# Both halves of a modulation row in one spread, and five reorderings of issue

## The chip, the cores and the metric

The kernel runs on one core of a Trainium2 chip. The metric is the device time of one execution in microseconds. Three runs of the kernel before gave 704.02, 704.18 and 706.19; the median is 704.18. One more execution was profiled.

The names of the profile: PE is TensorE's matmuls, PEld its weight loads, DVE is VectorE, ACT is ScalarE, POOL is GpSimd, SP is SyncE, which here issues DMAs. A "q" behind a name is the sequencer of that engine. Line numbers (L778) are lines of the kernel before.

## The reference

One layer of a decoder trunk on 512 tokens of width 1024, all in float32. A vector c gives six modulation rows: silu(c) times w_ada, a sum over 1024 rows of a matrix, plus a bias.

```python
mod = cs @ w_ada[l] + b_ada[l]
shift1, scale1, gate1, shift2, scale2, gate2 = split(mod, 6)
h = rmsnorm(x, norm1_g) * (1 + scale1) + shift1
qa, ka, va, qd, kd, vd, ga, gd = split(h @ w_in)
out_a = sliding_window_attention(qa, ka, va)       # 8 heads, window 128
out_d = diff_attention(qd, kd, vd)                 # 4 heads, two softmaxes, per-head norm
merged = sigmoid(ga) * (out_a @ w_branch_swa) + sigmoid(gd) * (out_d @ w_branch_diff)
x = x + gate1 * (merged @ w_out)
h2 = rmsnorm(x, norm2_g) * (1 + scale2) + shift2
a, g = split(h2 @ w_up)                            # 2 x 2816 columns
x = x + gate2 * ((gelu(causal_conv3(a) + conv_b) * g) @ w_down)
out = rmsnorm(x, final_g)
```

## The kernel before

**Precision.** Matrix products are made of three fp32r matmuls: a high part, rounded, and a low part, the rest, of both operands (high by high, high by low, low by high). So each weight and each activation is first split: a copy on ScalarE writes the high part, a subtraction on VectorE the low part. TensorE waits for the one that comes last, mostly the low part.

**The stages, in order of time.** The input is normalised and shift1 and scale1 are made (to about 60 us); the projection and, between its pieces, the two attentions run to about 317 us, with their gates and branch projections; the output projection to about 362; then "the merge", which closes the output projection, normalises again and opens the up projection; the up projection to about 590, by products of sums of quarter blocks named p1, m5, m6, p2, p3, m7, p4 (`mul_slot`, L1142, matmuls at L1150); the down projection by the same seven products, one pass of six groups each, in the order m1, m5, m6, p2, p3, m7, p4 (`multiply`, L1754, matmuls at L1759), and at the end the last residual and the final norm (`last_rows`, L1695).

**Modulation rows.** The other four rows (gate1, shift2, scale2, gate2) are made beside the attentions by VectorE. `ada_rows` (L764) is a generator: for each row `idx` and each half `hf` of 512 columns it goes through w_ada in four loads of two 128-row blocks (`ada_load`, L757, 512 KB each, issued by SyncE into one of the four buffers of `raw_tile`, L105, which the weights of the projections use too), and adds block times entry of silu(c) into a 128x512 tile `arow`: one multiply (L776) for the first block and a multiply-add (L778) for each of the other seven. The tile of half 0 has the tag `sq2`, that of half 1 the tag `g2b1`; each tag is one buffer. What is left is the sum over the 128 partitions. `ada_spread` (L785) does it with a matrix of ones on TensorE: four matmuls (L789), each with 32 columns of ones and 128 columns of `arow`, each at its own column tile of the array and into its own 32 partitions of a PSUM bank (`tbank`, L99, two banks shared with all transposes). ScalarE copies the result (L794), and a DMA from GpSimd (L795) writes one row of each 32 to DRAM, from where the rows are read later. A float32 matmul is two instructions in the profile, so a spread is eight.

`fill` (L489) issues pieces of projections between the steps of attention, and on each eighth call takes one step of `ada_rows`; `after` (L514) holds the spread back by one more call. From the 20th call on the operations of a row are given a higher priority than what is issued around them, but less than the row copy has. A scheduler then orders each engine's instructions by priority and dependence; each engine issues its own in that order. TensorE's order is written by hand in this part.

**The merge** (L1368 to L1480) and `last_rows` are written out by hand for all of TensorE, VectorE, ScalarE and GpSimd: the order of the lines is the order of issue on each engine. In the merge `sum_w`, `cast_w` and `low_w` (L1081 to L1093) make a sum of weight blocks (VectorE), its high part (ScalarE) and its low part (VectorE) for block column J; `turn2` (L1241) transposes the normalised input on TensorE, `mod_one` (L1250, activation at L1255) applies scale2 and shift2 to it on ScalarE; `mul_slot` is a product; `behind` (L1172) moves a product's result on (VectorE or ScalarE); `conv_taps` (L1159) is two multiply-adds of VectorE, `conv_gelu` an activation of ScalarE.

**The down projection** takes for each pass the six groups `g`, and for each group the two row blocks `u` of 128 tokens. The last pass, p4, holds its last three groups back for `last_rows`, which takes u = 0, then u = 1 in two halves of the columns, and closes the rows: multiply by the gate (L1671), add (L1674), square with its sum (L1677, ScalarE), multiply by the final gain (L1681), the power -1/2 on GpSimd (L173) between small VectorE steps (L171, L179, L183), and two scalings (L1688 on VectorE, L1692 on ScalarE), each with its output DMA.

Of the kernel before, what the change touches and what calls it, by code (L numbers as in the profile page):

```python
# [53 lines left out]
def kernel(  # L54
# [44 lines left out]
    def tbank(name, shape=(P, S)):  # L99
        return bank("t", 2, list(shape), name)  # L100
# [413 lines left out]
    def after(n, fn):  # L514
        later.append([n, fn])
# [241 lines left out]
    def ada_load(idx, hf, k):  # L757
        c0 = (2 + idx) * D + hf * S
        r = raw_tile([P, 2, S], f"ra{idx}{hf}_{k}")
        nc.sync.dma_start(r, wada[k * P : (k + 2) * P, c0 : c0 + S].rearrange("(a p) n -> p a n", p=P))  # L760
        return r


    def ada_rows():  # L764
        todo = [(idx, hf, k) for idx in range(4) for hf in range(2) for k in range(0, KT, 2)]
        r = ada_load(*todo[0])
        yield
        for (idx, hf, k), job in zip(todo, todo[1:] + [None]):
            nxt = ada_load(*job) if job else None
            if k == 0:  # L770
                ac = big.tile([P, S], F32, tag=("sq2", "g2b1")[hf], name=f"arow{idx}{hf}")
            with tc.high_priority(offset=HP // 2) if tick[0] > ADA_EASY else ExitStack():
                for a in range(2):
                    cc = cs[:, k + a : k + a + 1]
                    if k + a == 0:
                        nc.vector.tensor_scalar_mul(ac, r[:, a], cc)  # L776
                    else:
                        nc.vector.scalar_tensor_tensor(ac, r[:, a], cc, ac, ALU.mult, ALU.add)  # L778
            if k == KT - 2:
                after(ADA_LAG, lambda idx=idx, hf=hf, ac=ac: ada_spread(idx, hf, ac))  # L780
            r = nxt
            yield


    def ada_spread(idx, hf, ac):  # L785
        pr = tbank(f"pr{idx}{hf}", (P, P))
        for g in range(4):
            gs = slice(32 * g, 32 * g + 32)
            nc.tensor.matmul(  # L789
                pr[gs], ones[:, gs], ac[:, g * P : (g + 1) * P], start=True, stop=True, tile_position=(0, 32 * g)  # L790
            )
        row = big.tile([P, P], F32, tag="g2b0", name=f"row{idx}{hf}")
        with tc.high_priority(offset=HP):
            nc.scalar.copy(row, pr)  # L794
        nc.gpsimd.dma_start(  # L795
            mod_rows[idx, hf * S : (hf + 1) * S].rearrange("(g n) -> g n", g=4), row[0:P:32]
        )


    pair_w = {}  # L800
# [280 lines left out]
    def sum_w(J, name):  # L1081
        src = R[J, SRC[name]]
        nc.vector.tensor_add(src, src, R[J, "a11" if name == "m6" else "a12"])  # L1083

    def cast_w(J, name):
        W[J, name] = [
            wp.tile([P, 4, 256], F32R, tag=g, bufs=WB, name=f"{name}_{J}_{g}") for g in ("whi", "wlo")
        ]
        nc.scalar.copy(W[J, name][0], R[J, SRC[name]])  # L1089

    def low_w(J, name):
        hi, lo = W[J, name]
        nc.vector.tensor_sub(lo, R[J, SRC[name]], hi.bitcast(F32))  # L1093
# [61 lines left out]
    def conv_bias(J, u):  # L1155
        j = 2 * J + u
        nc.scalar.activation(grow(j), av[J][:, u], AF.Identity, bias=cv[:, 66 + j : 67 + j], scale=cv[:, 44 + j : 45 + j])  # L1157
# [92 lines left out]
    def mod_one(dst, tp, g, kk, on_vector=False):  # L1250
        k = 2 * g + kk
        if on_vector:
            nc.vector.tensor_scalar(dst[:, kk], tp[:, kk], a2c[:, k : k + 1], s2c[:, k : k + 1], ALU.mult, ALU.add)
        else:
            nc.scalar.activation(dst[:, kk], tp[:, kk], AF.Identity, bias=s2c[:, k : k + 1], scale=a2c[:, k : k + 1])  # L1255

    def ks(g):
        return slice(2 * (g % 2), 2 * (g % 2) + 2)
# [108 lines left out]
    g22 = pairs2.rearrange("p (b u n) -> p b u n", b=2, u=2)  # L1367
    tps = {g: turn2(2, g) for g in (0, 1)}  # L1368
    mul_slot(0, "p2", (0,))
    cast_w(0, "m5")  # L1370
    for g in (0, 1):
        for kk in range(2):
            mod_one(b12[:, ks(g)], tps[g], g, kk)
    for g in (2, 3):
        tps[g] = turn2(2, g)
    mul_slot(0, "p2", (1,))
    mul_slot(1, "p1", (1,))
    mul_slot(1, "p2")
    bV += [tbank("up6"), tbank("up7")]
    low_w(0, "m5")  # L1380
    for q in (q0, q1):
        V.tensor_sub(t1n[:, q], b11[:, q], b12[:, q])
    sum_w(0, "m6")
    hi_t(0, t1n, q0)
    for kk in range(2):
# [47 lines left out]
    mul_slot(1, "m6")  # L1433
    behind(1, "m5")
    conv_bias(0, 1)
    conv_taps(0, 0)
    sum_w(1, "p3")
    conv_taps(0, 1)
    cast_w(1, "p3")
    conv_gelu(0, 0)  # L1440
    behind(1, "m6")
    cast_w(1, "m7")
    low_w(1, "p3")
    mul_slot(1, "p3")
    conv_gelu(0, 1)
    low_w(1, "m7")
# [2 lines left out]
    cast_w(2, "p1")  # L1449
    behind(0, "c22")  # L1450
    behind(0, "p4")
    behind(1, "p2")
    low_w(2, "p1")
    mul_slot(2, "p1")
    behind(1, "p3")
    cast_w(1, "p4")
# [238 lines left out]
    def last_rows(todo):  # L1695
        man = ExitStack()
        man.enter_context(
            tc.manual_schedule(engines={nc.vector.engine, nc.scalar.engine, nc.tensor.engine, nc.gpsimd.engine})
        )
        c0, c1 = slice(0, H), slice(H, S)  # L1700
        part = [partial(parts[2 + u, 1]) for u in range(2)]
        for g in todo:
            multiply(len(passes) - 1, g, 0)
        for sl in (c0, c1):
            for g in todo:
                multiply(len(passes) - 1, g, 1, sl)
        for u in range(2):
            nc.scalar.activation(x1[:, u], x1[:, u], AF.Copy, scale=stat_end(u))
            nc.sync.dma_start(od[u * P : (u + 1) * P, :], x1[:, u])
        last_mul(0)  # L1710
        s0 = last_add(0)
        last_gain(0)
        last_mul(1, c0)
        r0 = rstd_start(s0, 1, D, bp, plus=part[0])
        s1 = last_add(1, c0)
        last_gain(1, c0)
        rs0 = bp.tile([P, 1], F32, tag="rs2", bufs=4, name="rse0")
        rstd_end(rs0, *r0, 1, bp)
        partial(s1, part[1])
        last_mul(1, c1)  # L1720
        s2 = last_add(1, c1)
        r1 = rstd_start(s2, 1, D, bp, plus=s1)
        last_gain(1, c1)
        last_scale(0, rs0)
        last_scale2(0, rs0, nc.sync)
        rs1 = bp.tile([P, 1], F32, tag="rs2", bufs=4, name="rse1")
        rstd_end(rs1, *r1, 1, bp)
        last_scale(1, rs1)
        last_scale2(1, rs1, nc.scalar)
        man.close()  # L1730
# [37 lines left out]
    for i in range(len(passes)):  # L1768
        for g in range(NG):
            prepare(i, g)  # L1770
            for _ in range(EACH.get(i, (0,) * NG)[g]):
                next(tasks)()
        tail = HOLD if i == len(passes) - 1 else 0
        for g in range(NG - tail):
            for u in range(2):
                multiply(i, g, u)
        if tail:
            last_rows(range(NG - tail, NG))
        else:
            tasks = after_pass(passes[i][0])  # L1780
            if i < 2:
                for _ in tasks:
                    pass
# [27 lines left out]
```

## Time and profile before

| | us |
|---|---|
| median of three runs | 704.18 |
| profiled execution | 704.88 |
| its span, first to last instruction | 703.0 |
| TensorE busy | 683.2 (97%) |
| VectorE busy | 571.9 (81%) |
| ScalarE busy | 375.5 (53%) |
| GpSimd busy | 82.3 (12%) |
| TensorE's mean granted clock | 0.994 |

How to read it. The profiled execution's own time is 1.9 us more than its span, and 0.70 more than the median. Lines of the timeline give start, duration, engine, line of the kernel, operation, output and inputs, shapes and, in brackets, how long the engine stood idle in front of it and which instruction ended that. A group line gives the operation, its count, its busy time, the mean of one in ns, and the idle time in front of the group. TensorE's matmuls overlap in the records: the step from start to start, not the duration, is what one costs.

### The profile page before, as it was taken

The page shows a single profiled execution, that of the slowest core. Times are in us where ns is not written, and L with a number is a line of the kernel's source. Part 1 is how long each engine was busy: PE and PEld are TensorE (multiplying, and loading weights), DVE is VectorE, ACT ScalarE, POOL GpSimd, SP SyncE. Part 2 cuts the span into 40 slices and gives each one's busy share as a digit, 9 for nine tenths or more (in the row PEclk, how much of TensorE's full clock was granted, in tenths as well). Part 3 has the DMA queues.
Part 4 walks back from the last instruction along what each step waited for, and adds up shares of the span by engine and source line. Part 5 has one row for each costly group of instructions (what it writes and reads, how often), then busy time and mean ns, then how long its engine had stood idle before and what let it go on. Part 6 is the DMA issues. An engine that isn't in the chain of part 4 may idle for free. (4 is left out here: it accounts for less than half of the span.)

```text
span 703.0 us, 11254 instructions
## 1 busy us (share of the span) xinstructions
PE 683.2 (97%) x4203; PEld 595.3 (85%) x4203; DVE 571.9 (81%) x1098; ACT 375.5 (53%) x668; POOL 82.3 (12%) x100
## 2 busy tenths in 40 slices
PE   6999999999999999999999999999999999999994
PEld 5777776778788888888889999999999999888884
DVE  5899886887885557664589898888888999979996
ACT  3646767455452333331468566655565666656664
POOL 3000000001001000000030111111111102530300
PEclk9999999999999999999999999999999999999998
DMA  9885454354435676229517798786889647996803
GB/s 312 282 260 174 150 151 151 92 170 128 134 108 158 194 225 202 96 106 275 185 44 149 188 212 204 169 206 194 197 213 231 156 148 204 196 198 192 157 1 119
DMA packets 115862, 121.81 MB, mean 173 GB/s; under 512 B 4383, under 2 KB 93280, under 8 KB 115808
## 3 DMA queue, kind: packets, MB, share of 16 engines
q1 hardware_dynamic: 96894, 95.09, 42.5%
q0 software_dynamic: 18720, 25.73, 21.7%
q8 instruction: 33, 0.54, 0.3%
q10 hardware_dynamic: 194, 0.28, 0.1%
q14 instruction: 21, 0.17, 0.1%
HBM read 118.97 MB, written 2.11 MB: 172 GB/s over the span
## 5 line engine op out<-in xcount | busy, mean ns | idle before, releaser
L1150 PE MATMUL up<-t,m_whi 128*128 128x256 f32 x528 | 96.1, 283 | 0.0
L1150 PEld LDWEIGHTS up<-t,m_whi 128*128 128x128 f32 x528 | 82.4, 192 | 0.0
L1150 PE MATMUL up<-t,m_wlo 128*128 128x256 f32 x264 | 74.7, 283 | 0.1
L1150 PE MATMUL up<-bh,p_wlo 128*128 128x256 f32 x232 | 65.7, 284 | 0.6 <-DVE p_wlo L1093 0.6
L1150 PE MATMUL up<-bh,p_whi 128*128 128x256 f32 x232 | 65.6, 283 | 0.0
L1150 PE MATMUL up<-bl,p_whi 128*128 128x256 f32 x232 | 65.6, 283 | 0.0
L778 DVE SCALAR_TENSOR_TENSOR arow<-ra,cs,arow 128x512 f32<-128x512 f32 x56 | 41.9, 748 | 21.7 <-DMA ra<-in_w_ada_dram 21.3
L1150 PEld LDWEIGHTS up<-t,m_wlo 128*128 128x128 f32 x264 | 50.6, 192 | 0.3 <-DVE m_wlo L1093 0.3
L1150 PEld LDWEIGHTS up<-bh,p_wlo 128*128 128x128 f32 x232 | 44.4, 192 | 1.0 <-DVE p_wlo L1093 1.0
L1150 PEld LDWEIGHTS up<-bl,p_whi 128*128 128x128 f32 x232 | 44.5, 192 | 0.0
L1150 PEld LDWEIGHTS up<-bh,p_whi 128*128 128x128 f32 x232 | 44.5, 192 | 0.0
L1061 POOL DMA_DIRECT2D s<-in_w_up_dram x21 | 27.0, 1360 | 143.2 <-DMA s<-in_w_up_dram 80.9
L1093 DVE TENSOR_TENSOR m_wlo<-s,m_whi 128x1024 fp32r<-128x1024 f32 x31 | 37.7, 1218 | 2.0 <-ACT m_whi L1089 2.0
L1089 ACT CAST m_whi<-s 128x1024 fp32r<-128x1024 f32 x31 | 32.4, 1046 | 9.4 <-DVE s L1083 5.9
L1150 PE MATMUL up<-t,p_whi 128*128 128x256 f32 x176 | 32.2, 283 | 0.0
L173 POOL TENSOR_TENSOR r<-ms,mhalf 128x1 f32<-128x1 f32 (+1 forms) x16 | 12.6, 788 | 134.3 <-DVE ms L171 75.7
L795 POOL DMA_DIRECT2D mod_rows<-row x8 | 5.1, 643 | 196.7 <-ACT row L794 196.7
L1150 PEld LDWEIGHTS up<-t,p_whi 128*128 128x128 f32 x176 | 27.4, 192 | 0.2 <-issue 0.2
L698 ACT ACTIVATE sd<-sd,dmx 128x128 f32<-128x128 f32 (+3 forms) x32 | 17.7, 556 | 18.5 <-DVE dmx L690 18.5
L1157 ACT ACTIVATE gT<-a,cv 128x512 f32<-128x512 f32 x22 | 17.7, 813 | 17.7 <-DVE a L1192 17.3
L1089 ACT CAST p_whi<-wa 128x1024 fp32r<-128x1024 f32 x18 | 18.7, 1040 | 12.0 <-PE up L1150 10.8
L1150 PE MATMUL up<-t,p_wlo 128*128 128x256 f32 x88 | 24.9, 283 | 0.0
(473 smaller groups left out, 2054.1 us busy)
## 6 DMA issues: line engine op xcount, KB each, us to landing
ra<-in_w_ada_dram SPq DMA_DIRECT2D x32, 512.0 KB, 3.9
wa<-in_w_up_dram SPq DMA_DIRECT2D x22, 512.0 KB, 4.1
s<-in_w_up_dram SPq DMA_DIRECT2D x21, 512.0 KB, 4.8
s<-in_w_up_dram POOLq DMA_DIRECT2D x21, 512.0 KB, 7.8
adaw<-in_w_ada_dram SPq DMA_DIRECT2D x16, 512.0 KB, 5.3
w<-in_w_in_dram SPq DMA_DIRECT2D x12, 512.0 KB, 4.0
a<-in_w_up_dram SPq DMA_DIRECT2D x11, 512.0 KB, 4.6
b<-in_w_down_dram SPq DMA_DIRECT2D x10, 512.0 KB, 3.5
```

The source lines that it names most:

```text
L173: nc.gpsimd.tensor_tensor(r0, ms, mhalf[:, :n], ALU.pow)
L698: exp = nc.scalar.activation(pm[m], pm[m], AF.Exp, bias=mx[:, m : m + 1], scale=slope, accum_out=lsum[:, m : m + 1])
L778: nc.vector.scalar_tensor_tensor(ac, r[:, a], cc, ac, ALU.mult, ALU.add)
L795: nc.gpsimd.dma_start(mod_rows[idx, hf * S : (hf + 1) * S].rearrange("(g n) -> g n", g=4), row[0:P:32])
L1061: nc.gpsimd.dma_start(dst, upblock(*blk), accum_op=ALU.add)
L1089: nc.scalar.copy(W[J, name][0], R[J, SRC[name]])
L1093: nc.vector.tensor_sub(lo, R[J, SRC[name]], hi.bitcast(F32))
L1150: nc.tensor.matmul(o[u], w[:, k, cu], b[:, k], start=name in ("p1", "m5", "p2") and k == 0 and x == 0, stop=k == 3 and x == 2, skip_group_ ...
L1157: nc.scalar.activation(grow(j), av[J][:, u], AF.Identity, bias=cv[:, 66 + j : 67 + j], scale=cv[:, 44 + j : 45 + j])
```

## The change

Six parts, in the order of the code.

1. `ada_spread` is called once for a row, behind its second half, with both halves. It issues eight matmuls, four for each half, into two 128-column pieces of one bank; the row copy is 128x256; two DMAs follow. The accumulation of each column tile is begun by the first half's matmul and closed by the second's.
2. In the merge, `cast_w(0, "m5")` goes behind the first of the two pairs of modulations.
3. There too, `low_w(0, "m5")` goes between the two halves of the t1n subtraction.
4. The sum, the high and the low part of (1, p3) go ahead of the convolution's taps, one pair of taps each; `low_w(2, "p1")` goes ahead of `behind(1, "p2")`.
5. In `last_rows` the norm of the third row block is closed, and its ScalarE scaling issued, before the last multiply; the two column halves of the fourth row block's multiply and add follow each other, and gains, the partial sum and the third block's VectorE scaling come behind.
6. In the last pass but one, m7, the last two groups are issued first for u = 0, then for u = 1.

```diff
@@ -763,6 +763,7 @@
 
     def ada_rows():
         todo = [(idx, hf, k) for idx in range(4) for hf in range(2) for k in range(0, KT, 2)]
+        sums = [None, None]
         r = ada_load(*todo[0])
         yield
         for (idx, hf, k), job in zip(todo, todo[1:] + [None]):
@@ -776,25 +777,29 @@
                         nc.vector.tensor_scalar_mul(ac, r[:, a], cc)
                     else:
                         nc.vector.scalar_tensor_tensor(ac, r[:, a], cc, ac, ALU.mult, ALU.add)
-            if k == KT - 2:
-                after(ADA_LAG, lambda idx=idx, hf=hf, ac=ac: ada_spread(idx, hf, ac))
+            sums[hf] = ac
+            if hf and k == KT - 2:
+                after(ADA_LAG, lambda idx=idx, acs=tuple(sums): ada_spread(idx, acs))
             r = nxt
             yield
 
 
-    def ada_spread(idx, hf, ac):
-        pr = tbank(f"pr{idx}{hf}", (P, P))
-        for g in range(4):
-            gs = slice(32 * g, 32 * g + 32)
-            nc.tensor.matmul(
-                pr[gs], ones[:, gs], ac[:, g * P : (g + 1) * P], start=True, stop=True, tile_position=(0, 32 * g)
-            )
-        row = big.tile([P, P], F32, tag="g2b0", name=f"row{idx}{hf}")
+    def ada_spread(idx, acs):
+        pr = tbank(f"pr{idx}", (P, 2, P))
+        for hf, ac in enumerate(acs):
+            for g in range(4):
+                gs = slice(32 * g, 32 * g + 32)
+                nc.tensor.matmul(
+                    pr[gs, hf], ones[:, gs], ac[:, g * P : (g + 1) * P], start=hf == 0, stop=hf == 1,
+                    tile_position=(0, 32 * g), skip_group_check=True,
+                )
+        row = big.tile([P, 2, P], F32, tag="g2b0", name=f"row{idx}")
         with tc.high_priority(offset=HP):
             nc.scalar.copy(row, pr)
-        nc.gpsimd.dma_start(
-            mod_rows[idx, hf * S : (hf + 1) * S].rearrange("(g n) -> g n", g=4), row[0:P:32]
-        )
+        for hf in range(2):
+            nc.gpsimd.dma_start(
+                mod_rows[idx, hf * S : (hf + 1) * S].rearrange("(g n) -> g n", g=4), row[0:P:32, hf]
+            )
 
 
     pair_w = {}
@@ -1367,19 +1372,20 @@
     g22 = pairs2.rearrange("p (b u n) -> p b u n", b=2, u=2)
     tps = {g: turn2(2, g) for g in (0, 1)}
     mul_slot(0, "p2", (0,))
-    cast_w(0, "m5")
     for g in (0, 1):
         for kk in range(2):
             mod_one(b12[:, ks(g)], tps[g], g, kk)
+        if g == 0:
+            cast_w(0, "m5")
     for g in (2, 3):
         tps[g] = turn2(2, g)
     mul_slot(0, "p2", (1,))
     mul_slot(1, "p1", (1,))
     mul_slot(1, "p2")
     bV += [tbank("up6"), tbank("up7")]
+    V.tensor_sub(t1n[:, q0], b11[:, q0], b12[:, q0])
     low_w(0, "m5")
-    for q in (q0, q1):
-        V.tensor_sub(t1n[:, q], b11[:, q], b12[:, q])
+    V.tensor_sub(t1n[:, q1], b11[:, q1], b12[:, q1])
     sum_w(0, "m6")
     hi_t(0, t1n, q0)
     for kk in range(2):
@@ -1433,14 +1439,14 @@
     mul_slot(1, "m6")
     behind(1, "m5")
     conv_bias(0, 1)
+    sum_w(1, "p3")
     conv_taps(0, 0)
-    sum_w(1, "p3")
+    cast_w(1, "p3")
+    low_w(1, "p3")
     conv_taps(0, 1)
-    cast_w(1, "p3")
     conv_gelu(0, 0)
     behind(1, "m6")
     cast_w(1, "m7")
-    low_w(1, "p3")
     mul_slot(1, "p3")
     conv_gelu(0, 1)
     low_w(1, "m7")
@@ -1449,8 +1455,8 @@
     cast_w(2, "p1")
     behind(0, "c22")
     behind(0, "p4")
+    low_w(2, "p1")
     behind(1, "p2")
-    low_w(2, "p1")
     mul_slot(2, "p1")
     behind(1, "p3")
     cast_w(1, "p4")
@@ -1710,19 +1716,19 @@
         last_mul(0)
         s0 = last_add(0)
         last_gain(0)
-        last_mul(1, c0)
         r0 = rstd_start(s0, 1, D, bp, plus=part[0])
-        s1 = last_add(1, c0)
-        last_gain(1, c0)
         rs0 = bp.tile([P, 1], F32, tag="rs2", bufs=4, name="rse0")
         rstd_end(rs0, *r0, 1, bp)
-        partial(s1, part[1])
+        last_scale2(0, rs0, nc.sync)
+        last_mul(1, c0)
+        s1 = last_add(1, c0)
         last_mul(1, c1)
         s2 = last_add(1, c1)
+        last_scale(0, rs0)
+        partial(s1, part[1])
         r1 = rstd_start(s2, 1, D, bp, plus=s1)
+        last_gain(1, c0)
         last_gain(1, c1)
-        last_scale(0, rs0)
-        last_scale2(0, rs0, nc.sync)
         rs1 = bp.tile([P, 1], F32, tag="rs2", bufs=4, name="rse1")
         rstd_end(rs1, *r1, 1, bp)
         last_scale(1, rs1)
@@ -1771,8 +1777,12 @@
             for _ in range(EACH.get(i, (0,) * NG)[g]):
                 next(tasks)()
         tail = HOLD if i == len(passes) - 1 else 0
-        for g in range(NG - tail):
+        twins = 2 if i == len(passes) - 2 else 0
+        for g in range(NG - tail - twins):
             for u in range(2):
+                multiply(i, g, u)
+        for u in range(2):
+            for g in range(NG - tail - twins, NG - tail):
                 multiply(i, g, u)
         if tail:
             last_rows(range(NG - tail, NG))
```

## The prediction

> **What bounds the kernel now.** I read the page from the top first. One engine is full: TensorE works through 97% of the span, VectorE through 81%. So only two things can move the time: TensorE instructions that come or go, and the places where TensorE stands and waits.
>
> ```profile
> PE 683.2 (97%) x4203; PEld 595.3 (85%) x4203; DVE 571.9 (81%) x1098; ACT 375.5 (53%) x668; POOL 82.3 (12%) x100
> ```
> ```profile
> L778 DVE SCALAR_TENSOR_TENSOR arow<-ra,cs,arow 128x512 f32<-128x512 f32 x56 | 41.9, 748 | 21.7 <-DMA ra<-in_w_ada_dram 21.3
> ```
>
> The second fence is the one to remember. The modulation rows cost VectorE 56 multiply-adds of 0.75 us, plus one short multiply of 0.48 at the head of each half, and before them VectorE already stands 21.3 us for their loads. That is slack only as long as these operations can start early.
>
> Next I read the waits of TensorE, and around each the timeline. The waits that the change touches are quoted below at their parts. All sums are made against the profiled execution (704.88 us, its span 703.0 of them), which is 0.70 above the median of the three runs, 704.18. About 0.3% (2.1 us) is what a measurement of this kernel can tell from no change.
>
> **Part 1, the spreads: what goes.** A spread is 8 short TensorE instructions (4 column tiles, two passes each) between ordinary matmuls. The first fence is the group of all eight spreads, the second one of them in the timeline:
>
> ```profile
> L789 PE MATMUL pr<-arow,ones x64: 272/285/298, 109.1 to 291.4; 128*32 128x128 f32 x64
> ```
> ```profile
> 222.22 0.39 PE L120 MATMUL pA<-outal,wba_h 128*128 128x512 f32 x1
> 222.45 0.39 PE L121 MATMUL pA<-outah,wba_l 128*128 128x512 f32 x1
> 222.77 0.43 PE L789 MATMUL pr<-arow,ones 128*32 128x128 f32 x8
> 223.12 0.50 PE L119 MATMUL pA<-outah,wba_h 128*128 128x512 f32 x1
> 223.46 0.39 PE L120 MATMUL pA<-outal,wba_h 128*128 128x512 f32 x1
> ```
>
> The usual step from one matmul to the next is 0.23 us (222.22 to 222.45). From 222.45 to 223.46 there would be two steps, 0.46; there are 1.01. A spread costs 0.55. Of the eight, four go, one at each first half. The four that stay get 8 more instructions. Their price isn't in the trace: it lies between nothing (they pack beside the others) and 0.55 (a second spread). I take 0.25, twice the 0.12 step of a 256-column matmul (396.88 to 397.00, quoted in part 2), because most of the 0.55 lies at the two edges. So three of the four pairs gain 0.30 each, 0.9 in all.
>
> The first pair is different, since the row copy of its first half stands in front of TensorE:
>
> ```profile
> 111.93 0.48 DVE L776 TENSOR_SCALAR arow<-ra,cs 128x512 f32<-128x512 f32 x1
> 112.17 0.26 ACT L794 COPY row<-pr 128x128 f32<-128x128 f32 x1
> 112.33 0.68 DVE L429 TENSOR_TENSOR qkv<-pv,qkv 128x512 fp32r<-128x512 f32 x1
> 112.49 0.42 PEld L595 LDWEIGHTS tp<-ident,st 128*128 128x128 f32 x4 [1.07 <-ACT row L794]
> ```
>
> TensorE waits for that copy (1.07 in front of the weight load of its transposes), and four transposes later for the qkv low part, which ends at 113.01. Without the copy the second wait is next: its VectorE operation moves up by the arow multiply in front of it (0.40), so the gain is 0.40, not 1. With the larger spread at 136.07 behind it TensorE stands at -0.15.
>
> **Part 1, what it adds: a wait.** The row of a first half lies in a tile with one buffer. Before, the 111.93 multiply could begin the next index's row as soon as the first half had been spread, at 109. Now both halves are read by one spread at 136.07, so in the changed kernel's order of issue this multiply, the two multiply-adds on each of the loads, and all loads that wait for buffers that they release, stand behind it. VectorE issues in order; what is queued behind is the softmax of the diff attention, for which TensorE waits.
>
> ```profile
> 136.07 0.42 PE L789 MATMUL pr<-arow,ones 128*32 128x128 f32 x8
> ```
> ```profile
> DMA to landing us min/median/max: 3.6/3.7/4.1
> ```
> ```profile
> 140.77 0.28 DVE L680 CUSTOM_DVE_ANT_0 sd<-sd,ddf 128x128 f32<-128x128 f32 x1
> ```
> ```profile
> 145.55 0.30 PE L716 MATMUL td<-ident,sd 128*128 128x128 f32 x1
> ```
>
> **Stall A.** The larger spread ends at 136.07 - 0.40 + 0.42 + 0.25 = 136.35, the multiply 0.5 later at 136.9, the first multiply-add at 137.65. This frees the load buffer for the third load of the row, which lands 3.7 later (second fence), at 141.4. Its multiply-add (to 142.2) stands ahead of the scores of query block 1, which started at 140.77 and took 1.27 with their maxima; now they end at 143.4. Between them and the L704 operation that ends them before the transpose at 145.55 the new order has, besides that chain's own small steps (L690, L701, L702 at 0.16 each, 0.3 and 0.35 for L703 and L704, 0.68 for an aTl): three multiply-adds of 0.75 and one multiply of 0.48. That is 4.5, less 0.08 of overlap at each of ten seams, 3.7: 147.1. The transpose starts 0.1 later, 147.2 in place of 145.55: TensorE is at +1.65.
>
> **Stall B.** The scores of query block 2 need the low part of the new keys:
>
> ```profile
> 160.73 0.68 DVE L429 TENSOR_TENSOR qkv<-pk,qkv 128x512 fp32r<-128x512 f32 x1
> 161.33 0.47 DVE L703 TENSOR_SCALAR sd<-sd,dls 128x512 f32<-128x512 f32 x1
> 161.72 0.55 DVE L429 TENSOR_TENSOR aTl<-td,aTh 128x384 fp32r<-128x384 f32 x1
> 162.19 0.74 DVE L704 SCALAR_TENSOR_TENSOR sd<-sd,dls,sd 128x512 f32<-128x512 f32 x1
> ```
> ```profile
> 161.81 0.44 PE L126 MATMUL sd<-qkv 64*128 64x128 f32 x4
> ```
> ```profile
> 150.05 1.23 DVE L116 TENSOR_TENSOR w_l<-w,w_h 128x1024 fp32r<-128x1024 f32 x1 [0.91 <-ACT w_h L115]
> ```
>
> Before, the low part ends at 161.41 and TensorE wants it at 161.98 (the later matmuls of the second fence). In the new order the three operations behind it in the first fence stand ahead of it (1.5 with overlaps), and so do two multiply-adds more than before (2 x 0.67). This stretch starts at the weight split of 150.05 (third fence), for which VectorE already stood waiting on ScalarE, which follows TensorE there; so it starts 1.65 late. The low part ends at 161.41 + 1.65 + 1.5 + 1.35 = 165.9, TensorE starts at 166.1: +4.1, of which 2.45 are new. The later three pairs give back 0.9. In the stages of the third and fourth row I followed the new order by the same durations and found no wait that ends after TensorE's own arrival, though some by only 0.6 us. Part 1: **+3.2**.
>
> The low point of TensorE's activity in B may cost more than its length:
>
> ```profile
> 11.40:14.80 3.40, 1.43 (x13) 0.99 1.10 349
> 14.80:18.10 3.30, 3.30 (x16) 0.50 1.09 350
> ```
>
> These are stretches of the start: length, TensorE busy, granted clock. After 3.4 us with 1.43 busy and no single gap over 1.5 the clock was halved for the next 3.3. The Trainium skill, "TensorE: Matmul & The Clock Gate", section "HAM oscillation — how this bites in real kernels", asks for more: idle of over about 3.4 us. By that page B stays free of charge; by this row it might not. I keep it out of the sum and make it a rival.
>
> **Part 2, the merge.** Moving the cast of m5 behind the first pair of modulations takes away what ScalarE did while it waited for TensorE's transposes:
>
> ```profile
> 367.00 1.03 PE L1245 MATMUL th<-ident,xn 128*128 128x128 f32 x8
> ```
> ```profile
> 367.30 1.03 ACT L1089 CAST m_whi<-s_t 128x1024 fp32r<-128x1024 f32 x1
> 368.24 1.91 ACT L1255 ACTIVATE braw<-th,c 128x256 f32<-128x256 f32 x4
> ```
> ```profile
> 370.20 0.66 PE L1245 MATMUL th<-ident,xn 128*128 128x128 f32 x4 [0.25 <-ACT braw L1255]
> ```
> ```profile
> 391.05 0.48 PE L1150 MATMUL up<-t,p_whi 128*128 128x256 f32 x2
> ```
>
> The first four of the eight transposes are there at about 367.6; ScalarE, free at 367.3, then idles some 0.3, and the cast's full 1.03 falls between the two pairs. The last modulation ends 0.35 later, and so does the transpose at 370.20. The t1n and low operations of VectorE follow, with no gap up to the operation that the matmul at 391.05 waits for; it is 0.6 late: +0.6 instead of nothing. In return, three waits shrink:
>
> ```profile
> 396.88 0.28 PE L1150 MATMUL up<-bh,p_whi 128*128 128x256 f32 x1
> 397.00 0.28 PE L1150 MATMUL up<-bl,p_whi 128*128 128x256 f32 x1
> 397.58 0.39 PE L1150 MATMUL up<-bh,p_wlo 128*128 128x256 f32 x1 [0.31 <-DVE p_wlo L1093]
> ```
> ```profile
> 400.31 0.40 PE L1150 MATMUL up<-t,m_whi 128*128 128x256 f32 x2
> 400.82 0.39 PE L1150 MATMUL up<-t,m_wlo 128*128 128x256 f32 x1
> ```
> ```profile
> 403.68 0.28 PE L1150 MATMUL up<-bl,p_whi 128*128 128x256 f32 x1
> 404.29 0.39 PE L1150 MATMUL up<-bh,p_wlo 128*128 128x256 f32 x1 [0.32 <-DVE p_wlo L1093]
> ```
>
> Start to start beyond the 0.12 step: 0.47, 0.27 (two matmuls in the row) and 0.48. The low part of p3 moves ahead of two taps of 0.75, that of p1 ahead of several 0.33 steps of the closing work of p2, both more than the waits, so they go whole: -1.22. Part 2: **-0.6**.
>
> **Part 3, the end.** Finishing one row block of m7 early ends the wait of p4 for the subtraction:
>
> ```profile
> 678.63 0.47 PE L1759 MATMUL dc<-p4wh,p4a 128*128 128x512 f32 x1 [0.19 <-DVE chain_outl L1633]
> ```
> ```profile
> 694.73 0.65 POOL L173 TENSOR_TENSOR r<-ms,mhalf 128x1 f32<-128x1 f32 x1 [16.07 <-DVE ms L171]
> 697.69 0.62 POOL L173 TENSOR_TENSOR r<-ms,mhalf 128x1 f32<-128x1 f32 x1 [2.30 <-DVE ms L171]
> ```
>
> 678.63 moves to 678.28, a step of 0.23: TensorE ends 0.35 earlier. That isn't passed on: the third row block's power (694.73) now goes first, and its inputs, fixed by VectorE, let it end at about 693.9; two small steps later, at 694.2, the last multiply starts, against 694.10 before. From there multiply, add, multiply, add stand back to back (0.45 each), the last square starts at 696.0 against 696.84, and the second power and all behind it follow 0.85 to 0.95 earlier. Part 3: **-0.9**.
>
> Sum: +3.2 - 0.6 - 0.9 = **+1.7**, 706.6 in the profiled execution's terms, 705.8 against the median.
>
> **The rivals.**
> 1. *Neither stall comes.* The loads land before VectorE needs them or it catches up, as its 21.3 us of standing would allow. Then part 1 is -0.4 + 0.25 - 0.9 = -1.05, the whole -2.6: 701.6. Against: the wait on the spread is a matter of one buffer, and the in-order sum leaves no room.
> 2. *A comes, B doesn't* (the low part isn't held up because the split at 150 isn't late): part 1 is +1.65 - 0.9 = +0.75, whole -0.75: 703.4.
> 3. *The clock is halved after B.* Slower on the other side: if the idle 2.45 us at 163.5 to 166 fall in one window of the clock's gate, 3.3 us at half speed add 1.65: 707.5. It decides from where TensorE's work in 3.4 us falls to some 40%, as in the row of the start; B leaves 28%. For it: that row. Against: there the work was mostly transposes, and B may be split between two windows.
> 4. *A third stall* in the later rows, where 0.6 us are spare and each row again starts late: 1 to 2 us more, 707.3.
>
> **How the numbers follow.** Forecast (704.9 to 706.7) 0.40; rival 1: 0.18; rival 2: 0.12; rival 3: 0.16; rival 4: 0.14. The likeliest case gives 705.8. Slower by over 0.3% begins at 706.3: rivals 3 and 4 and a quarter of the forecast, 0.40. Faster begins at 702.1: rival 1 less its upper edge, 0.16. The rest, 0.44, is the same. The range takes in rivals 1 and 3 at their prices: 701.4 to 708.0. The unknown price of the larger spread moves the sum from -1.0 to +1.2 by its bounds, inside it.
>
> **What would show it.** In the changed kernel's profile: eight spreads become four, of 16 instructions and about 0.8 us each; VectorE's first arow multiply after the spread at 136; a TensorE wait at td L716 near 147 of over 1 us, and one at sd L126 near 164 to 166 of over 2, both released by VectorE; the waits on p_wlo gone, one of 0.6 more at the p4 matmul near 394; the last power almost 1 us nearer to the last matmul. I am wrong if TensorE shows no wait between 137 and 170, or if its granted clock falls there.

## The result, and the profile after

The changed kernel is slower: six runs gave 707.01 to 709.64 us, median 709.01, against a median of 704.4 (704.02 to 706.19) of six runs of the kernel before. The measured ratio is 1.0047, or +3.3 us, with a 95% interval of 1.0027 to 1.0067; the quotient of the two medians, 1.0065, lies at its upper end. Run again beside the experiments it gave 1.0045 (1.0027 to 1.0063), 1.0059 (1.0045 to 1.0074) and 1.0068 (1.0050 to 1.0086): some 3 to 5 us.

The profiled execution is the fastest of the six, 707.01, span 705.2. First TensorE's waits; columns: the line that waits, what for, us in total, times, the longest.

```profile
PE sd L126 <- DVE qkv L429: 2.4, 1, 2.4
...
PE td L716 <- DVE dls L701: 1.8, 1, 1.8
PE th L1250 <- DVE xn L1240: 1.5, 1, 1.5
...
PE tp L595 <- DVE qkv L429: 1.1, 1, 1.1
...
PE th L1250 <- ACT braw L1260: 0.7, 1, 0.7
...
PE up L1155 <- DVE pairs L1195: 0.3, 1, 0.3
PE up L1155 <- DVE m_wlo L1098: 0.2, 1, 0.2
```

The first two are the stalls B and A of the prediction. The third, at 361, is not in it. `tp` is the small wait that takes the place of the one on the row copy. The last three lie in the merge: two that the prediction has, and one (`m_wlo`) that it hasn't. The waits on `p_wlo` and on `chain_outl` are gone.

The page's lines for the engines and for the row's multiply-adds:

```profile
PE 680.2 (96%) x4203; PEld 593.9 (84%) x4203; DVE 572.0 (81%) x1098; ACT 376.3 (53%) x664; POOL 82.6 (12%) x100
...
L779 DVE SCALAR_TENSOR_TENSOR arow<-ra,cs,arow 128x512 f32<-128x512 f32 x56 | 41.8, 747 | 16.4 <-DMA ra<-in_w_ada_dram 16.0
```

TensorE has the same number of instructions and is busy for 3 us less, and the span is 2.2 longer. VectorE is busy for as long as it was; it stands 5.3 us less in front of these operations, nearly all of it less waiting for their loads (16.0 in place of 21.3).

The stretch of stall A, in TensorE's and then in VectorE's timeline:

```profile
134.70 0.65 PE L792 MATMUL pr<-arow,ones 128*32 128x128 f32 x16
```
```profile
135.19 0.49 DVE L777 TENSOR_SCALAR arow<-ra,cs 128x512 f32<-128x512 f32 x1 [0.75 <-PE pr L792]
135.72 0.75 DVE L779 SCALAR_TENSOR_TENSOR arow<-ra,cs,arow 128x512 f32<-128x512 f32 x1
```
```profile
143.61 0.73 DVE L779 SCALAR_TENSOR_TENSOR arow<-ra,cs,arow 128x512 f32<-128x512 f32 x1
144.25 0.15 DVE L702 TENSOR_TENSOR dls<-dls,nlam 128x1 f32<-128x1 f32 x1
144.32 0.48 DVE L777 TENSOR_SCALAR arow<-ra,cs 128x512 f32<-128x512 f32 x1
144.72 0.28 DVE L703 TENSOR_SCALAR sd<-sd,dls 128x128 f32<-128x128 f32 x1
144.92 0.74 DVE L779 SCALAR_TENSOR_TENSOR arow<-ra,cs,arow 128x512 f32<-128x512 f32 x1
145.58 0.34 DVE L704 SCALAR_TENSOR_TENSOR sd<-sd,dls,sd 128x128 f32<-128x128 f32 x1
```
```profile
146.07 0.30 PE L716 MATMUL td<-ident,sd 128*128 128x128 f32 x1 [1.78 <-DVE dls L701]
```

The row's first multiply is released by the spread; nine us later its followers stand between the small steps L702, L703 and L704, and the transpose waits for the last of them. (The profile names the releaser one step early: L704 ends at 145.92.) Stall B has the same shape:

```profile
161.52 0.74 DVE L779 SCALAR_TENSOR_TENSOR arow<-ra,cs,arow 128x512 f32<-128x512 f32 x1
162.19 0.48 DVE L703 TENSOR_SCALAR sd<-sd,dls 128x512 f32<-128x512 f32 x1
162.58 0.55 DVE L429 TENSOR_TENSOR aTl<-td,aTh 128x384 fp32r<-128x384 f32 x1
163.05 0.74 DVE L704 SCALAR_TENSOR_TENSOR sd<-sd,dls,sd 128x512 f32<-128x512 f32 x1
163.71 0.74 DVE L779 SCALAR_TENSOR_TENSOR arow<-ra,cs,arow 128x512 f32<-128x512 f32 x1
164.37 0.68 DVE L429 TENSOR_TENSOR qkv<-pk,qkv 128x512 fp32r<-128x512 f32 x1
```
```profile
165.11 0.61 PE L126 MATMUL sd<-qkv 64*128 64x128 f32 x6 [2.45 <-DVE qkv L429]
```

Where the time went is read best from the starts of the same TensorE instruction in two traces. The table has the change of (start after minus start before) over each stretch; times at the left are those of the kernel before. "Again" is the changed kernel in its three further profiles (e1, e9, e12 below).

| stretch | forecast | after | again |
|---|---|---|---|
| 0 to 99, where nothing is changed | 0 | -0.95 | -2.05, -1.54, -1.65 |
| 99 to 137, first pair of spreads | -0.15 | -0.19 | -0.09, -0.10, -0.10 |
| 137 to 145.6, stall A | +1.8 | +1.65 | +1.74, +1.72, +1.91 |
| 145.6 to 150.5 | 0 | 0 | 0, 0, +1.52 |
| 150.5 to 162.0, stall B | +2.45 | +2.61 | +2.44, +2.67, +2.35 |
| 162.0 to 165.4 | -0.55 | -0.44 | +1.10, +1.13, +1.07 |
| 165.4 to 300, the other spreads | -0.35 | -0.27 | +0.27, -0.10, +0.30 |
| 350 to 359, the first of the merge | 0 | +1.61 | 0, 0, 0 |
| 359 to 413.5, the merge | -0.6 | -0.35 | -0.37, -0.35, -0.38 |
| 600 to the end of the span | -0.9 | -1.48 | -1.42, -1.41, -1.43 |

The first row is a trap: the profiled execution of before was 1 to 2 us slower in a part that no kernel here changes than all others, and so its span flatters whatever it is compared with. From 99 on, the four profiles of the changed kernel are 3.15, 3.65, 3.5 and 5.25 us longer.

### The profile page after: what moved, and what is told of

Its sections match the earlier page's. It is cut to its first block, busy times and chain, and to the rows that moved or that the text cites. A ratio compares the mean times of both kernels' runs of the same rounds, so it can differ in the third digit from the quotient of the medians.

```text
span 705.2 us, 11250 instructions
## 1 busy us (share of the span) xinstructions
PE 680.2 (96%) x4203; PEld 593.9 (84%) x4203; DVE 572.0 (81%) x1098; ACT 376.3 (53%) x664; POOL 82.6 (12%) x100
```

## The experiments

All ratios are against the kernel before on the same chip.

**e1, e9 and e12: the changed kernel again**, without an edit, beside the others.

> The changed kernel once more, for a second profile and its spread. The profiled run of 707.01 was the fastest of six (the others 708.0 to 709.6) at the highest mean clock (0.996 against 0.990 to 0.995). Theory W (the waits of the diff attention at 146 and 165 are the loss) expects both waits again, 1.7 and 2.6 us more than before. Theory C (after the second wait the clock is halved for about 3.3 us in most executions) expects a stretch of clock 0.50 within 4 us behind 165 if this profile's execution is one of the slow ones. Rival L (a load that lands 2 us late holds the merge at 361) expects the wait of 1.5 us at 361 again; if it was an accident of one execution, it is gone. Time: 708.5 to 709.5.

Measured: 706.31 us (705.63 to 709.17) where the kernel before has 703.21; 1.0045 (1.0027 to 1.0063), less than the 708.5 to 709.5 that was expected. The two waits are there, the one at 361 isn't. Theory C shows in the profile. Columns: stretch, length, TensorE busy and instructions, granted clock, DMA share, GB/s.

```profile
161.00:164.50 3.50, 1.23 (x12) 1.00 0.58 156
164.50:165.00 0.50, 0.50 (x7) 0.74 0.64 170
165.00:168.00 3.00, 3.00 (x9) 0.50 0.48 143
168.00:169.00 1.00, 1.00 (x7) 0.92 0.00 0
```

Behind stall B the clock is halved for 3.4 us: nine instructions in 3 us, where the profile of after, which has no halving, has 21:

```profile
165.00:168.00 3.00, 2.89 (x21) 1.00 0.67 186
```

> The changed kernel beside the next kernel on the same chip, since the clock's part in the loss is not settled: the filled version had a mean clock of 0.992 to 0.998 against 0.990 to 0.997, but no better time. Expected: clock 0.990 to 0.993 in most runs, and where a run has 0.996 or more, 1 us less.

Measured: 707.74 us (706.83 to 709.94), before 703.38; 1.0059 (1.0045 to 1.0074). Two of the six runs have a clock of 0.990 or 0.991 (709.94, 708.34), the others 0.994 or 0.995 (706.83 to 708.21); a low clock was expected in most. Its profile has the halved clock behind B.

> The changed kernel beside it: 1.0045 to 1.0060 times the kernel before, mean clock 0.990 to 0.993 in at least half of the runs.

Measured: 708.65 us (705.23 to 709.58), before 703.36; 1.0068 (1.0050 to 1.0086). Five runs have a clock of 0.990 to 0.992 (708.14 to 709.58), one has 0.997 (705.23). The ratio is over the expected 1.0045 to 1.0060. Here the clock was halved behind stall A too, which the table shows as +1.52:

```profile
142.00:145.70 3.70, 1.67 (x8) 1.00 0.53 159
146.00:149.50 3.50, 3.50 (x14) 0.52 0.82 239
150.00:153.00 3.00, 3.00 (x18) 1.00 0.64 196
```

Over all 24 runs of the changed kernel, the 14 with a mean clock of 0.992 or less have a median of 708.9, the 7 with 0.995 or more 707.0.

**e2, e10 and e11: work of no use in the waits.** Matmuls whose result is overwritten are put where TensorE stands; e10 has the second group alone.

```diff
         tp = tbank(f"td{h}_{n}")
+        if (h, n) == (1, 0):
+            for _ in range(6):
+                nc.tensor.matmul(tp, heads[1][:, 0, :P], heads[1][:, 0, :], start=True, stop=True)
...
+            if (h, n) == (2, 0):
+                for _ in range(17):
+                    nc.tensor.matmul(firsts[h][0]..., heads[1][:, 0, :P], heads[1][:, 0, :256], start=True, stop=True)
             mm3_rows([
```

> The changed kernel with matmuls of no use put into TensorE's two waits: 6 of 512 columns ahead of the transposes at 146, 17 of 256 columns ahead of the scores at 165 (1.4 and 2.0 us of work into banks that the next instructions overwrite). They fit into the idle time, so by theory W alone the time is that of the changed kernel, within 0.4 us. By theory C the clock isn't halved any more: 1.7 to 2.5 us faster than the changed kernel on the same chip, and a mean clock of 0.994 to 0.996 in every run.

Measured: 707.9 us (706.2 to 709.23); 1.0057 (1.0042 to 1.0072), so 1.6 over the changed kernel of that chip. Five runs have a clock of 0.994 to 0.998 and one 0.992, and the profile has no halving behind either wait, nearly as theory C expects; the time is not. In this trace a multiply-add of the row, held up by its load, starts 5.3 us after the load's issue, where the traces of the changed kernel have 4.5 to 4.7; stall B is some 0.8 longer, and the wait at 361 is there.

> The changed kernel with the useless matmuls ahead of the scores at 165 alone. Theory C: no halved clock behind 165, mean clock 0.994 or more, and 1.0 to 1.3 us faster than the changed kernel beside it (what the two halved stretches in the traces added to TensorE's delay). If the times are the same again, what the clock costs there is taken back later (the waits behind it are for loads and VectorE, not for TensorE), and the halved clock is no part of the loss.

Measured: 705.78 us (704.92 to 707.71), beside 707.74 of the changed kernel, so 2.0 less where 1.0 to 1.3 was expected; 1.0030 (1.0019 to 1.0042). Six of the eight runs have a clock of 0.994 or more. In its profile the clock is whole behind B and halved behind A, which wasn't filled.

> The version with useless matmuls at both waits again, since the two fillings contradict each other: with both waits filled 1.0057 times the kernel before (on its chip 1.6 us over the changed kernel), with the second alone 1.0030 (on its chip 2.0 us under it). Theory C: the first of the two was an accident of late loads (in its trace one load of the row landed 1 us later than usual, and the one at 345 took 6 us); now 1.5 to 2.5 us under the changed kernel beside it. If it is again at or over the changed kernel, the filling of the first wait itself costs, and the clock's part stays open.

Measured: 706.5 us (704.85 to 707.83), beside 708.65 of the changed kernel; 1.0041 (1.0027 to 1.0056). All clocks are 0.994 to 0.998, and the profile has no halving behind either stall:

```profile
161.00:164.50 3.50, 2.94 (x22) 1.00 0.54 154
164.50:168.00 3.50, 3.31 (x23) 1.00 0.57 163
```

So theory C holds in two of the three pairs, at 2 us each: more matmuls made the kernel faster, and what the traces show as gained is the clock. The profiles of e10 and e11 give a part of it back, 1.05 and 1.44 us, at a later wait (rival 4 below). The first pair speaks against theory C, and its late loads are a reason that its trace shows for one execution, not for six.

**e3: the spread alone.** All edits outside `ada_rows` and `ada_spread` are undone.

```diff
-            if k == KT - 2:
-                after(ADA_LAG, lambda idx=idx, hf=hf, ac=ac: ada_spread(idx, hf, ac))
+            sums[hf] = ac
+            if hf and k == KT - 2:
+                after(ADA_LAG, lambda idx=idx, acs=tuple(sums): ada_spread(idx, acs))
```

> The kernel before with the one spread for each row alone, the merge and the end as before. Theory W: both waits, TensorE 3.3 us later at 295 than before, and the time 3.3 us over before; with theory C 5 to 6 over before in most runs. Rival M (the reorderings of the merge are the loss) expects no more than 1 us over before.

Measured: 709.18 us (708.11 to 710.96), before 703.21; 1.0079 (1.0065 to 1.0094). By its trace TensorE is 4.9 us later at 300 than the difference at 99, of which the halved clock behind B is 1.5. Theory W with theory C; rival M falls.

**e5: everything but the spread.** The other way round.

> The changed kernel without part 1: two spreads for each row as before, the merge and the end as changed. From the difference of the changed kernel and the spread alone on one chip (706.3 against 709.2): 2.9 us faster than before. From the traces alone (merge -0.35 between 357 and 413, the end -1.4): 1.7 faster. No wait at 146 and 165, no halved clock there, mean clock as before.

Measured: 701.88 us (700.98 to 703.0), before 703.21, so 1.3 less; 0.9979 (0.9969 to 0.9989). The trace gives -0.37 in the merge and -1.45 at the end. It is the sum of the traces, 1.7, that nearly held, not the difference of the two medians, 2.9.

**e4 and e8: a tile of its own for every other row.** The wait is taken away by another buffer, within the space that there is: the half 0 of odd rows takes the tile that the row copies had, and each row copy goes into the tile of the half that the spread has just read.

```diff
-                ac = big.tile([P, S], F32, tag=("sq2", "g2b1")[hf], name=f"arow{idx}{hf}")
+                ac = big.tile([P, S], F32, tag=("sq2" if idx % 2 == 0 else "g2b0", "g2b1")[hf], name=f"arow{idx}{hf}")
...
-        row = big.tile([P, 2, P], F32, tag="g2b0", name=f"row{idx}")
+        row = big.tile([P, 2, P], F32, tag="sq2" if idx % 2 == 0 else "g2b0", name=f"row{idx}")
```

> The changed kernel in which the half 0 of every other row has a tile of its own (the one that the row copies had, which go into the tile of the row just read). So the next row's first multiply needn't wait for the spread of both halves. Theory W: no wait at 146 and 165, the spreads' gain of about 1 us remains, and with merge and end the whole is 2.5 us faster than before: 701.9, and the mean clock is that of before. Rival (the larger spread itself costs): still slower than before.

Measured: 700.16 us (699.82 to 701.33); 0.9954 (0.9941 to 0.9966).

> The version with a tile of its own for every other row once more, beside the one without the two edits on the same chip: 3.0 us faster than before again (2.5 by the sum of the traces); its profile shows whether the wait at 361 comes here too (rival L: it has nothing to do with the spread), or not.

Measured: 700.7 us (699.87 to 701.05); 0.9957 (0.9941 to 0.9974). Neither profile has a wait of `td` or `sd`, and the clock is whole from 137 to 300. The spreads now give what they were priced at: from 99 to 300 TensorE gains 0.7 and 1.0 us. The changed kernel and e4, on one chip, are 6 us apart by the tags of two tiles.

**e6: ordinary priority.** The wait stays, and only the place of the multiply-adds in VectorE's order changes.

```diff
-            with tc.high_priority(offset=HP // 2) if tick[0] > ADA_EASY else ExitStack():
+            with ExitStack():
```

> The changed kernel with the row's multiplies and multiply-adds at ordinary priority. They still wait for the spread of both halves, but no longer stand ahead of the softmax and of the low part of the keys in VectorE's order: in the order of issue the low part of qkv2 is ahead of the three operations again and of both multiply-adds of the last load, and one multiply less stands ahead of the transpose. Theory W in its narrow form (the place in VectorE's order is what costs, not the wait as such): the first wait shrinks to some 0.5 to 1 us, the second is gone, 702 to 703 on a chip on which the changed kernel has 706 to 707 and the kernel before 703 to 704. Rival (the late rows cost wherever they stand, by loads and buffers): 705 or more, with new waits of TensorE between 170 and 300.

Measured: 704.4 us (702.36 to 705.0), before 703.21; 1.0005 (0.9994 to 1.0016), between the 702 to 703 of theory W and the 705 of its rival. The second wait is gone as expected, the first has grown instead of shrinking:

```profile
PE td L716 <- DVE dls L701: 2.6, 1, 2.6
```
```profile
142.31 1.21 DVE L116 TENSOR_TENSOR w_l<-w,w_h 128x1024 fp32r<-128x1024 f32 x1
143.44 0.15 DVE L702 TENSOR_TENSOR dls<-dls,nlam 128x1 f32<-128x1 f32 x1
143.50 0.75 DVE L779 SCALAR_TENSOR_TENSOR arow<-ra,cs,arow 128x512 f32<-128x512 f32 x1
144.17 0.28 DVE L703 TENSOR_SCALAR sd<-sd,dls 128x128 f32<-128x128 f32 x1
144.36 0.75 DVE L779 SCALAR_TENSOR_TENSOR arow<-ra,cs,arow 128x512 f32<-128x512 f32 x1
145.03 0.35 DVE L704 SCALAR_TENSOR_TENSOR sd<-sd,dls,sd 128x128 f32<-128x128 f32 x1
```

A weight split of 1.21 us that stood behind the transpose's chain in the changed kernel now stands in front, and two of the row's multiply-adds still stand in it. The place in the order does cost, but at A the ordinary priority doesn't keep the row's operations out of the chain. In this profile the clock stayed whole behind a wait of 2.56 us.

**e7: the best of it.** The tiles of e4, without the two edits of the merge that the traces show as a loss.

```diff
+    cast_w(0, "m5")
     for g in (0, 1):
         for kk in range(2):
             mod_one(b12[:, ks(g)], tps[g], g, kk)
-        if g == 0:
-            cast_w(0, "m5")
...
-    V.tensor_sub(t1n[:, q0], b11[:, q0], b12[:, q0])
     low_w(0, "m5")
-    V.tensor_sub(t1n[:, q1], b11[:, q1], b12[:, q1])
+    for q in (q0, q1):
+        V.tensor_sub(t1n[:, q], b11[:, q], b12[:, q])
```

> The kernel with a tile of its own for every other row, without the two edits of the merge that the traces show as a loss (the cast of m5 behind the first modulations, +0.4 at 370; the t1n subtraction ahead of the low part of m5, with it +0.2 at 391). Expected 0.4 to 0.6 us faster than the version that keeps them: 3.5 us faster than before. If these two edits aren't the cause of the 0.6, it is as fast as that version, 3.0 faster than before.

Measured: 699.38 us (698.83 to 701.23); 0.9947 (0.9930 to 0.9964), beside 700.7 of e8: 1.3 less, where 0.4 to 0.6 was expected. The wait of `th` on `braw` is 0.3 again, that of `up` on `pairs` is gone, and the merge gains 0.94 where it gained 0.36 in e8: the traces give 0.6 of the difference. It has the lowest median here, 3.8 us under that of the kernel before.

## Why the prediction was right, and where it wasn't

**The time.** The sum was +1.7 us, with a range of 701.4 to 708.0. By the measured ratio it is +3.3 us, 707.5 in the terms of the median of 704.18; the median of the six runs, 709.01, is over the upper end. So the direction is right, with 0.40 for slower by over 0.3%, and the sum is half of what came. That 707.5 lies within the range is owed to rival 3, which the range takes in, and not to the sum.

**Part 1** was right in its two stalls. The waits are where they were put, and these sizes came within 0.25: -0.15 became -0.09 to -0.19, stall A +1.8 became +1.65 to +1.9, stall B +2.45 became +2.35 to +2.7. The unknown price of the larger spread, taken as 0.25, shows as steps of 0.20 to 0.26 at three of the four spreads. e4 shows that the single buffer is the cause: with a second one both waits go and nothing else is needed. Rivals 1 and 2 fall; the gain that rival 1 priced at 2.6 for a kernel without the stalls is near what e4 and e8 measured, 2.5 and 3.05 by the medians.

**The step that failed** is the one that left the clock out of the sum: "By that page B stays free of charge; by this row it might not. I keep it out of the sum and make it a rival." Rival 3, given 0.16, is what three of four profiles of the changed kernel show: the clock was halved behind B in these and in that of e3, and behind A, which no rival had, in e12. That is also one of the two signs that the prediction names for being wrong, a granted clock that falls between 137 and 170. It costs 1.5 us each time by the traces (1.1 beside the -0.44 of the same stretch without it) and 2 by e10 and e11. The row of the start was a better guide than the rule: no idle stretch in front of these halvings is over 2.55 us.

Why the same wait did it in some executions and not in others can be read from the starts of the halved stretches. Where one execution has two of them before 200 us (14.56 and 164.74 in e1, 14.79 and 164.97 in e3, 13.76 and 146.88 in e10, 146.12 and 166.60 in e12), they lie 44, 44, 39 and 6 times 3.413 us apart. So in each of these traces the clock changes on a fixed grid of 3.413 us, and the grid lies elsewhere in each execution.

Cut along its own grid (found, where there is no other halving, from the one at the end of the trace), a trace has a wait in one interval or divided between two. Between 100 and 320 us, in all profiles, the six intervals with 1.00 to 1.56 us of TensorE's work are followed by a halved one (B in e1, e3, e9 and e12, A in e12 and e10), and none with more is: the next are 1.63 behind A in the profile of after, 1.85 in e6, 1.94 behind B in the profile of after and 1.95 behind A in e9. Whether a limit between 1.56 and 1.63 is the whole rule no run here shows; at the start of the kernel this count doesn't separate them (2.04 in e11 is followed by a halved interval, 1.46 in e9 isn't). "B may be split between two windows", which the prediction holds against rival 3, is what the profile of after shows: 2.44 and 1.94 of work in the two intervals that share its 2.45 us of waiting. Its other reason, that the work at the start was mostly transposes, misreads that row: of its 13 instructions two are transposes (`xt`).

**Rival 4**, a third stall in the later rows, came smaller than its 1 to 2 us, and part 1's "no wait that ends after TensorE's own arrival" failed there. At the matmul that starts at 223.92 in the kernel before, TensorE loses 0.52 us in e1, 0.29 in e9, 0.64 in e12 and nothing in the profile of after. From e12:

```profile
226.74 0.75 DVE L779 SCALAR_TENSOR_TENSOR arow<-ra,cs,arow 128x512 f32<-128x512 f32 x1 [4.78 <-DMA ra<-in_w_ada_dram]
227.41 0.68 DVE L747 TENSOR_TENSOR of<-of,rb 128x512 f32<-128x512 f32 x1
228.12 0.62 ACT L115 CAST outdA<-of 128x512 fp32r<-128x512 f32 x1 [1.13 <-DVE of L747]
228.64 0.59 ACT L811 ACTIVATE ta<-pga 128x512 f32<-128x512 f32 x1
229.29 0.50 PE L119 MATMUL pga<-hThA,wga_h 128*128 128x512 f32 x1 [0.48 <-ACT ta L811]
```

A multiply-add of the late row waits for its load at the head of VectorE's order; behind it stand an operation of the attention's output, its high part on ScalarE, and the activation that TensorE waits for. That is why the stretch from 165.4 to 300 gained less than forecast, or lost.

Another stall came in one of the four profiles, at 361, where the prediction didn't look for it. The loads in front of the merge landed late:

```profile
DMA to landing us min/median/max: 4.8/6.5/7.3
```

In e1 the same ten loads have a median of 5.1. The profile of e2 has this wait too, and that of e11 a smaller one of 0.5 us; those of e1, e3, e4 to e10 and e12 don't have it, or only 0.2. The one spread for each row doesn't bring it by itself, then. But 0.5 us or more came only with the stalls of the joined spread, in three of nine profiles, and in none of those of e4, e5, e7 and e8, which are too few to tell. What makes these loads late in some executions stays open.

**Part 2** had each of its terms nearly right and missed one. In this fence are, from the profile of after, the two waits that were to grow, the matmul on p3's low part, and one that wasn't in the sum:

```profile
374.62 0.44 PE L1250 MATMUL th<-ident,xn 128*128 128x128 f32 x2 [0.67 <-ACT braw L1260]
...
395.68 0.48 PE L1155 MATMUL up<-t,p_whi 128*128 128x256 f32 x2 [0.26 <-DVE pairs L1195]
...
401.74 0.28 PE L1155 MATMUL up<-bh,p_wlo 128*128 128x256 f32 x1
...
416.85 0.39 PE L1155 MATMUL up<-t,m_wlo 128*128 128x256 f32 x1 [0.20 <-DVE m_wlo L1098]
```

Against the kernel before the two waits cost 0.42 and 0.23, the forecast 0.6. The three low parts give -0.57, -0.37 and -0.58, each 0.1 more than forecast with the step behind it. TensorE, now 1.5 earlier against VectorE, then loses 0.44 at 416.85, where it waits for a low part that came just in time before. VectorE's work had only been moved behind, and more than a quarter of the gain came back at the next place where it is late. This gives -0.35 instead of -0.6.

**Part 3** was right in its mechanism and too small, -1.4 for -0.9:

```profile
681.73 0.40 PE L1765 MATMUL dc<-m7wh,m7a 128*128 128x512 f32 x1
681.96 0.40 PE L1765 MATMUL dc<-p4wh,p4a 128*128 128x512 f32 x1
```
```profile
697.11 0.22 DVE L179 SCALAR_TENSOR_TENSOR rt<-r,ms 128x1 f32<-128x1 f32 x1 [0.73 <-POOL r L173]
697.36 0.16 DVE L183 SCALAR_TENSOR_TENSOR rse<-rt,r 128x1 f32<-128x1 f32 x1
697.43 0.42 DVE L1677 TENSOR_TENSOR pairs<-dc,g2b 128x256 f32<-128x256 f32 x1
```
```profile
701.88 0.38 ACTq L1699 DMA_DIRECT2D out_dram<-x  x1
```

The wait for `chain_outl` is gone (a plain step of 0.23), and the last multiply does start behind the third block's norm, as forecast. The step that failed is "That isn't passed on": TensorE's 0.35 were passed on to the norm's inputs. The multiply is 3.34 later than before (697.43 against 694.10), while TensorE was 3.68 later in front of the pass: -0.34, not +0.1. From there to the last issue (701.88, before 699.55) it takes 4.45 instead of 5.45, -1.0.

**The sum** of the three parts, without the clock and the stall at 361, comes to +1.5 to +2.25 in the four profiles (forecast +1.7): from 3.15 take the 1.6 of the late loads; from 3.65, 3.5 and 5.25 the 1.5, 1.5 and 3.0 of the clock. That the rest agrees so well is in part luck, since misses cancel: part 3 gave 0.5 more than its forecast, the merge 0.25 less, and the stall at 224 took 0.3 to 0.6 in three profiles. What is over the forecast is the clock's in three of these profiles and the late loads' in one.

## What to carry to other kernels

- Joining two reductions into one keeps both operands alive until the later one: look at what waits for the earlier operand's buffer before counting the instructions that go. In an in-order engine, work that is held up and then released stands in front of somebody else's chain.
- An idle stretch of TensorE has to be priced by what it does to the granted clock as well: here about 2.4 us of waiting cost 1.5 us more in four of five profiles (B in after, e1, e3, e9, e12).
- Before comparing spans, compare the stretch in which nothing was changed.

## What the runs showed of the hardware

- The clock was halved for 3.4 us behind intervals of 3.413 us in which TensorE worked 1.00 to 1.56 us, without any idle stretch over 2.55 us. The section of the Trainium skill on the clock ("TensorE: Matmul & The Clock Gate", "HAM oscillation — how this bites in real kernels") speaks of idle gaps over about 3.4 us; these traces put the limit lower.
- Two halvings of one execution start a whole number of times 3.413 us apart (6, 39, 44 and 44 in e12, e10, e1 and e3), and the grid lies elsewhere in each execution: the same wait halved the clock where one interval held most of it, and not where two shared it.
- Matmuls of no use in such a wait made the kernel 2 us faster in two of three pairs (e10, e11).
- A load of 512 KB took 3.6 us from issue to landing in one execution and 6.2 in another at the same place of the same program (the load of `wa` issued at 345.4 in e9 and at 344.1 in the profile of after).
